# Which of four weight buffers each multiply of a feed-forward part reads: in turn, or 0, 1, 2, 3, 1, 2, 3

## The chip, the cores and the metric

The kernel runs on one core of one Trainium2 chip. The metric is the device time of one execution in microseconds (us); less is better. The engines are named PE (TensorE), DVE (VectorE), ACT (ScalarE), POOL (GpSimd) and SP (SyncE, which here only issues transfers).

## The reference

One layer of a decoder with 512 tokens and a width of 1024. A token mixer (forgetting attention beside a state-space branch, joined by gates) comes first; the change lies behind it, in the SwiGLU part:

```python
x = layer_norm(DEEPNORM_ALPHA * x + mixed, ln1_g[l], ln1_b[l])
h = (jax.nn.silu(x @ w_ffn_gate[l]) * (x @ w_ffn_up[l])) @ w_ffn_down[l]
x = layer_norm(DEEPNORM_ALPHA * x + h, ln2_g[l], ln2_b[l])
```

`w_ffn_gate` and `w_ffn_up` are 1024 x 2816, `w_ffn_down` is 2816 x 1024, all float32.

## The kernel before, in words

**Splits.** A float32 product is made of three faster ones. `split` (lines 103 and 104) makes of a tile a high part (a cast on ACT, `...h`) and a low part (the rest, a subtraction on DVE, `...l`). `mm3` (lines 145 to 147) issues high x high, high x low and low x high.

**The feed-forward part.** The hidden width is cut into six blocks, five of 512 columns and one of 256. For each block the gate product and the up product are a `Gemm` object each (G0, U0 for the first block, up to G5, U5). A `Gemm` does a 2 x 2 block product with seven multiplies instead of eight: P1, P2, P6, P5, P7, P3, P4, in this order in the steady part. Each has its own right operand, made once from the transposed rows of x (`RIGHT`: B11, B21, NT2, NT1, T3, B22, T4), and its own weights: a quarter of the weight block, or a sum of quarters. The right operands are tiles of 128 x 1024, read in pieces of 128 x 256. One multiply is `nj` x 4 x 3 matmuls: 24 in the first five blocks, 12 in the sixth. There are 12 x 7 = 84 multiplies.

**The weights' way.** `load` (line 875) brings quarters from HBM into eight slots `rq`; where a sum of two quarters is wanted, POOL issues a second, accumulating load (line 877), or DVE adds (lines 883 and 885, for P6 and P3). `op` then splits the quarter into one of four buffers, each a pair `wh`, `wl`. `nops` counts the operations, and the buffer is the count modulo four. Buffers 0 and 1 lie in a pool that opens early (`wop0`), 2 and 3 in one that opens after the output projection (`wop1`). `W_OFF` (line 35) puts 192 bytes ahead of buffers 1 and 2, and none ahead of 0 and 3. A buffer may be written again when the multiply that read it is over.

**Order.** Engines other than SP and POOL follow what a scheduler makes of the code, which knows the buffers' dependencies. The opening is written out by hand: G0 and U0 take turns (numbers 0 to 13: G0 P1, G0 P2, U0 P1, U0 P2, G0 P5, U0 P5, G0 P6, U0 P6, G0 P7, G0 P3, G0 P4, U0 P7, U0 P3, U0 P4). From number 12 on a loop runs through `rest`, in which the split for a multiply is recorded two multiplies ahead of it (`AHEAD`). The numbers of G1 to U5 are 14 to 83; G5 and U5, numbers 70 to 83, are the halves.

**Behind it.** The down projection (`gemm_down`) loads `w_ffn_down` in chunks into `raw` (line 126) and splits them into `whi`, `wlo`. The `raw` tiles lie where slots of `rq` were, so that SP's first such load waits until the last split has read its slot.

Of the kernel before, what the change touches and what calls it, by code (L numbers as in the profile page):

```python
# [42 lines left out]
def tile_hybrid_decoder_layer(  # L43
# [47 lines left out]
    def offset(p_, n, nm):  # L91

        if n:
            p_.tile([P, n // 4], F32, name="off" + nm)
# [7 lines left out]
    def split(hi, lo, src):  # L102
        nc.scalar.copy(out=hi, in_=src)  # L103
        nc.vector.tensor_tensor(out=lo, in0=src, in1=hi.bitcast(F32), op=ALU.subtract)  # L104
# [725 lines left out]
    nops = [0]  # L830
# [18 lines left out]
    class Gemm:  # L849
# [29 lines left out]
        def op(self, p_):  # L879

            r = self.raw
            if p_ == "P6":
                nc.vector.tensor_tensor(out=r["a11"], in0=r["s1"], in1=r["a11"], op=ALU.add)
            elif p_ == "P3":
                nc.vector.tensor_tensor(out=r["a12"], in0=r["a11"], in1=r["a12"], op=ALU.add)
            t = r[{"P1": "a11", "P2": "a12", "P6": "a11", "P5": "s1", "P7": "s3", "P3": "a12", "P4": "a22"}[p_]]
            i = nops[0] % 4
            wp, off = wpools[i]
            if nops[0] < 4:
                offset(wp, off, f"w{i}")  # L890
            nops[0] += 1
            o = [wp.tile([P, 1024], F32R, name="w" + x, tag=f"w{x}{i}", bufs=1)[:, 0:4 * self.F] for x in "hl"]
            if nops[0] == 2:
                offset(wp, W_OFF[4], "we")
            split(*o, t)
            self.ops[p_] = [self.v(i) for i in o]
# [254 lines left out]
```

## Time and profile before

| | us |
|---|---|
| median of 3 runs | 1131.83 (1131.39 to 1133.82) |
| the profiled execution | 1133.8 |
| its span on the core | 1132.1 |

| engine | busy us | share of the span |
|---|---|---|
| PE | 1104.3 | 98% |
| DVE | 777.6 | 69% |
| ACT | 526.7 | 47% |
| POOL | 134.4 | 12% |

Time is counted from the start of the span. The feed-forward multiplies begin at 784 us, the down projection at 1002.5 us. A row of the timeline gives start, duration, engine, line, operation, `out<-in`, shape and a count; brackets hold the engine's idle time before it and what ended that. Tile names stand without buffer numbers: `wh` and `wl` are any of the four buffers. A matmul's duration reaches over the next one's start, since they are pipelined, so PE's pace is read from the starts.

### The profile page before, as it was taken

How to read it: one execution, taken by the hardware profiler on the slowest of the kernel's cores; microseconds unless marked ns; L12 is line 12 of the kernel's file. 1: busy time of each engine (PE TensorE's matmuls, PEld its weight loads, DVE VectorE, ACT ScalarE, POOL GpSimd, SP SyncE). 2: the span in 40 equal slices, each digit the busy share in tenths (PEclk: the TensorE clock that was granted, in tenths of full speed). 3: DMA queues.
4: the chain of work that ended last, by engine and by line, in shares of the span. 5: the costliest groups of instructions: out<-in, count | busy, mean ns of one | idle time of the engine just before them, and what ended most of it. 6: DMA issues, size and time to landing. Idle time of an engine off the chain costs nothing.

```text
span 1132.1 us, 15815 instructions
## 1 busy us (share of the span) xinstructions
PE 1104.3 (98%) x6086; PEld 942.8 (83%) x6086; DVE 777.6 (69%) x1223; ACT 526.7 (47%) x912; POOL 134.4 (12%) x165
## 2 busy tenths in 40 slices
PE   7999999999999999999999999999999999999996
PEld 5887778777787878888888888888999999988885
DVE  2679973885688473788778744556997777777326
ACT  2477764454442341567566544313654555453210
POOL 3003130020114000122110000011111111100001
PEclk9999999999999999999999999999999999999999
DMA  6353243243231333321222135381788787565212
GB/s 198 111 169 108 84 128 93 75 124 100 75 94 59 94 91 93 91 61 57 75 75 75 57 114 184 101 214 42 210 197 208 184 204 159 103 233 176 93 56 75
DMA packets 116059, 134.20 MB, mean 119 GB/s; under 512 B 5668, under 2 KB 94480, under 8 KB 115856
## 3 DMA queue, kind: packets, MB, share of 16 engines
q1 hardware_dynamic: 98896, 111.75, 32.3%
q0 software_dynamic: 14640, 14.10, 7.6%
q10 hardware_dynamic: 2448, 7.34, 1.9%
q8 instruction: 48, 0.79, 0.3%
q14 instruction: 27, 0.22, 0.1%
HBM read 128.78 MB, written 4.26 MB: 118 GB/s over the span
## 4 chain that ended last, share of the span: by engine, by line
PE 80%; DVE 9%; issue 4%; DMA 3%; POOL 2%; ACT 2%; POOLq 0%; DVEq 0%; ACTq 0%
PE gps L147 19%; PE gps L146 19%; PE gps L145 19%; PE cps L146 5%; PE cps L147 5%; PE cps L145 4%; PE cps L509 2%; DVE wlo L104 2%; PE cps L370 1%; PE cps L499 1%; ACT whi L103 1%; DMA rq<-in_w_ffn_up_dram 1%; PE cps L474 1%; PE cps L475 1%; PE cps L328 1%
## 5 line engine op out<-in xcount | busy, mean ns | idle before, releaser
L104 DVE TENSOR_TENSOR wlo<-raw,whi 128x1024 fp32r<-128x1024 f32 x127 | 156.2, 1230 | 176.4 <-ACT whi L103 175.1
L103 ACT CAST whi<-raw 128x1024 fp32r<-128x1024 f32 x127 | 133.5, 1051 | 244.3 <-PE gps L146 97.8
L145 PE MATMUL gps<-xh,whi 128*128 128x512 f32 x456 | 180.9, 397 | 0.0
L147 PE MATMUL gps<-xh,wlo 128*128 128x512 f32 x456 | 179.6, 394 | 0.0
L146 PE MATMUL gps<-xl,whi 128*128 128x512 f32 x456 | 179.3, 393 | 0.0
L103 ACT CAST wh<-rq 128x1024 fp32r<-128x1024 f32 (+1 forms) x84 | 82.1, 979 | 94.5 <-PE cps L146 42.7
L104 DVE TENSOR_TENSOR wl<-rq,wh 128x1024 fp32r<-128x1024 f32 (+1 forms) x84 | 94.8, 1132 | 29.5 <-ACT wh L103 29.3
L147 PEld LDWEIGHTS gps<-xh,wlo 128*128 128x128 f32 x456 | 86.1, 189 | 17.5
L145 PEld LDWEIGHTS gps<-xh,whi 128*128 128x128 f32 x456 | 86.0, 189 | 17.3 <-issue 0.2
L146 PEld LDWEIGHTS gps<-xl,whi 128*128 128x128 f32 x456 | 86.0, 189 | 17.3 <-issue 0.2
L145 PE MATMUL gps<-whi,xh 128*128 128x512 f32 x192 | 76.3, 398 | 1.9 <-ACT whi L103 1.6
L146 PE MATMUL gps<-wlo,xh 128*128 128x512 f32 x192 | 75.6, 394 | 1.2 <-DVE wlo L104 1.2
L147 PE MATMUL gps<-whi,xl 128*128 128x512 f32 x192 | 75.5, 393 | 0.0
L282 DVE SCALAR_TENSOR_TENSOR t_v<-gps,cw,t_v 128x511 f32<-128x511 f32 (+2 forms) x72 | 53.4, 744 | 3.8 <-ACT t_v L279 3.1
L146 PE MATMUL gps<-t_ul,whi 128*128 128x512 f32 x128 | 51.1, 399 | 0.0
L147 PE MATMUL gps<-t_uh,wlo 128*128 128x512 f32 x128 | 51.0, 399 | 0.0
L145 PE MATMUL gps<-t_uh,whi 128*128 128x512 f32 x128 | 50.5, 395 | 0.0
L481 ACT ACTIVATE t_y<-t_y,sm 128x128 f32<-128x128 f32 (+1 forms) x64 | 35.6, 558 | 21.1 <-DVE sm L479 21.0
L145 PEld LDWEIGHTS gps<-whi,xh 128*128 128x128 f32 x192 | 36.4, 190 | 10.5 <-ACT whi L103 2.3
L146 PEld LDWEIGHTS gps<-wlo,xh 128*128 128x128 f32 x192 | 36.4, 190 | 9.4 <-DVE wlo L104 2.0
L364 ACT ACTIVATE t_ab<-t_ab,acum 128x128 f32<-128x128 f32 x128 | 41.6, 391 | 4.7 <-DMA t_ab<-ac_d 2.7
L147 PEld LDWEIGHTS gps<-whi,xl 128*128 128x128 f32 x192 | 36.3, 189 | 8.5 <-DVE xl L104 1.1
(567 smaller groups left out, 2717.0 us busy)
## 6 DMA issues: line engine op xcount, KB each, us to landing
raw<-in_w_in_dram SPq DMA_DIRECT2D x80, 512.0 KB, 3.7
rq<-in_w_ffn_gate_dram SPq DMA_DIRECT2D x25, 512.0 KB, 5.9
rq<-in_w_ffn_up_dram SPq DMA_DIRECT2D x25, 512.0 KB, 6.3
raw<-in_w_ffn_down_dram SPq DMA_DIRECT2D x22, 512.0 KB, 3.8
t_ab<-ac_d SPq DMA_DIRECT2D x32, 256.0 KB, 3.2
raw<-in_w_proj_ssm_dram SPq DMA_DIRECT2D x16, 512.0 KB, 3.5
rq<-in_w_ffn_gate_dram POOLq DMA_DIRECT2D x10, 512.0 KB, 8.4
rq<-in_w_ffn_up_dram POOLq DMA_DIRECT2D x10, 512.0 KB, 6.2
```

What stands on the lines that cost most here:

```text
L103: nc.scalar.copy(out=hi, in_=src)
L104: nc.vector.tensor_tensor(out=lo, in0=src, in1=hi.bitcast(F32), op=ALU.subtract)
L145: nc.tensor.matmul(out=o, lhsT=l[0], rhs=r[0], start=start, stop=False, skip_group_check=skip)
L146: nc.tensor.matmul(out=o, lhsT=l[0], rhs=r[1], start=False, stop=False, skip_group_check=skip)
L147: nc.tensor.matmul(out=o, lhsT=l[1], rhs=r[0], start=False, stop=stop, skip_group_check=skip)
L282: nc.vector.scalar_tensor_tensor(out=v[:, sh:], in0=ps[:, 0:T - sh], scalar=cw[:, k, blk:blk + 1], in1=v[:, sh:], op0=ALU.mult, op1=ALU.add)
L328: nc.tensor.transpose(out=pt[:, c * P:(c + 1) * P], in_=xst[:, c * P:(c + 1) * P], identity=ident)
L364: nc.scalar.activation(out=m[:, r, :], in_=m[:, r, :], func=AF.Relu, scale=-1.0, bias=acum[:, c, h:h + 1])
L370: nc.tensor.matmul(out=py[:, r * 64:(r + 1) * 64], lhsT=ms[r // 4][:, r % 4, :], rhs=xdt[:, r * 64:(r + 1) * 64], start=True, stop=True)
L474: nc.tensor.matmul(out=ps[:, 0:n], lhsT=q1[:, qs], rhs=k1[:, 0:n], start=True, stop=False)
L481: nc.scalar.activation(out=pt[:, 0:n], in_=pt[:, 0:n], func=AF.Exp, scale=-1.0, bias=sm[:, 2:3], accum_out=sm[:, 0:1])
L509: nc.tensor.matmul(out=po[:, kb * P:], lhsT=vt[:, kb, hh, :], rhs=pT[kb][j], start=kb == 0 and j == 0, stop=kb == NT - 1 and j == 1)
```

## The change

The buffer of an operation is no longer its count modulo four. With seven operations to a `Gemm`, the pattern has its period: P1 gets buffer 0, P2, P6 and P5 get 1, 2, 3, and P7, P3 and P4 get 1, 2, 3 again.

```diff
@@ -884,7 +884,7 @@
             t = r[{"P1": "a11", "P2": "a12", "P6": "a11", "P5": "s1", "P7": "s3", "P3": "a12", "P4": "a22"}[p_]]
-            i = nops[0] % 4
+            i = (0, 1, 2, 3, 1, 2, 3)[nops[0] % 7]
             wp, off = wpools[i]
             if nops[0] < 4:
                 offset(wp, off, f"w{i}")
```

The scheduler sees other dependencies and so places some instructions anew. ACT, in the opening, from the split of B11 and B21 on (`b11h`, `nt1h`, `b22h`, `nt2h` are high parts of right operands, line 982 normalises rows):

```order
 L103 CAST b11h<-xf 128x1024
 L103 CAST b21h<-xf 128x1024
-L103 CAST wh<-rq 128x1024 x3
-L900 COPY cp<-gps 128x512
-L103 CAST wh<-rq 128x1024
+L103 CAST wh<-rq 128x1024 x2
+L900 COPY cp<-gps 128x512
+L103 CAST wh<-rq 128x1024 x2
 L982 ACTIVATE xf<-cps,lnv 128x128 x8
 L952 ACTIVATE g<-cp 128x512
 L103 CAST wh<-rq 128x1024
 L900 COPY cp<-cps 128x512
+L103 CAST nt1h<-T 128x1024
```

The cast of `nt1h` now stands right behind the copy, ahead of that of `b22h`, which it followed. DVE at the same place (lines 1037 and 1040 make NT1 and NT2, lines 986 and 987 normalise, line 953 is a gate's evacuation):

```order
-L953 SCALAR_TENSOR_TENSOR g<-g,cp 128x512
+L1037 TENSOR_TENSOR T<-xf 128x1024
 L987 TENSOR_TENSOR xf<-xf,lnv 128x4x128
-L1037 TENSOR_TENSOR T<-xf 128x1024
-L104 TENSOR_TENSOR wl<-rq,wh 128x1024
+L953 SCALAR_TENSOR_TENSOR g<-g,cp 128x512
 L1040 SCALAR_TENSOR_TENSOR T<-T,xf 128x1024
 L104 TENSOR_TENSOR nt1l<-T,nt1h 128x1024
```

The low part `wl` that leaves this place is that of U0's P5. It comes back as the first of three behind `nt2l` and the product of line 959. In PE's row the first four matmuls of G0's and U0's P6 now stand behind the first two of U0's P5, which do not need that low part. PE at the start of the down projection (`T` is the hidden tile, `whi` and `wlo` the first chunk):

```order
 L146 MATMUL cps<-t4l,wh 128x256
 L147 MATMUL cps<-t4h,wl 128x256
-L145 MATMUL cps<-whi,T 128x512 x3
+L145 MATMUL cps<-whi,T 128x512 x4
+L146 MATMUL cps<-wlo,T 128x512
+L147 MATMUL cps<-whi,T 128x512
+L145 MATMUL cps<-whi,T 128x512
```

Four matmuls that need only the high part of the chunk now stand ahead of the first that needs its low part, instead of three.

## Rows read from the trace of the kernel before

**Rows 1.** Span and granted clock of the core.

```profile
core 0: 1132.1 us, clock 0.996
```

**Rows 2.** Stretches: length, busy time of each engine, clock, DMA share, GB/s.

```profile
core 0: us, PE busy (x) PEld busy (x) DVE busy (x) ACT busy (x) POOL busy (x), PEclk, DMA share, GB/s
...
804.00:830.00 26.00, 26.00 (x227) 26.00 (x226) 26.00 (x29) 16.02 (x20) 2.58 (x2) 1.00 0.84 211
830.00:983.00 153.00, 153.00 (x1332) 153.00 (x1332) 119.85 (x130) 79.21 (x97) 21.85 (x17) 1.00 0.75 178
...
1002.50:1110.00 107.50, 107.22 (x474) 88.47 (x474) 51.10 (x48) 30.58 (x30) 0.00 (x0) 1.00 0.41 136
```

**Rows 3.** PE's waits, 784 to 1016 us: total, times, longest.

```profile
PE gps L146 <- DVE nt1l L104: 1.0, 1, 1.0
PE cps L979 <- DVE t_sd L971: 0.9, 1, 0.9
PE gps L145 <- ACT nt1h L103: 0.6, 1, 0.6
PE cps L146 <- DVE wlo L104: 0.3, 1, 0.3
```

**Rows 4.** PE by stretch, cut at the starts of multiplies 15, 16, 18 and 20.

```profile
831.42:834.14 2.72, 2.72 (x26) 1.00 0.63 165
834.14:837.02 2.88, 2.88 (x26) 1.00 1.21 218
...
839.74:842.46 2.72, 2.72 (x26) 1.00 1.21 229
...
845.18:848.06 2.88, 2.88 (x26) 1.00 0.16 55
```

**Rows 5.** Timeline of ACT, then DVE, from 837 us: splits of weights.

```profile
837.15 1.05 ACT L103 CAST wh<-rq 128x1024 fp32r<-128x1024 f32 x1 [0.48 <-PE gps L146]
...
838.23 1.23 DVE L104 TENSOR_TENSOR wl<-rq,wh 128x1024 fp32r<-128x1024 f32 x1 [0.50 <-ACT wh L103]
840.95 1.23 DVE L104 TENSOR_TENSOR wl<-rq,wh 128x1024 fp32r<-128x1024 f32 x1 [1.50 <-ACT wh L103]
```

**Rows 6.** Timeline of ACT, DVE, SP and PE at the hand-over, 995 to 1004 us.

```profile
995.79 0.62 ACT L103 CAST wh<-rq 128x512 fp32r<-128x512 f32 x1 [0.47 <-ACT cp L900]
...
996.73 0.69 DVE L104 TENSOR_TENSOR wl<-rq,wh 128x512 fp32r<-128x512 f32 x1
...
997.45 1.90 SPq L126 DMA_DIRECT2D raw<-in_w_ffn_down_dram  x4
...
1001.31 1.05 ACT L103 CAST whi<-raw 128x1024 fp32r<-128x1024 f32 x1 [2.28 <-DMA raw<-in_w_ffn_down_dram]
...
1002.39 1.23 DVE L104 TENSOR_TENSOR wlo<-raw,whi 128x1024 fp32r<-128x1024 f32 x1
...
1002.54 0.86 PE L145 MATMUL cps<-whi,T 128*128 128x512 f32 x3
1003.68 0.50 PE L146 MATMUL cps<-wlo,T 128*128 128x512 f32 x1 [0.28 <-DVE wlo L104]
```

**Rows 7.** Timeline of ACT, DVE and PE in the opening, 797 to 801 us.

```profile
797.35 1.05 ACT L103 CAST b22h<-xf 128x1024 fp32r<-128x1024 f32 x1
798.30 1.04 ACT L103 CAST nt1h<-T 128x1024 fp32r<-128x1024 f32 x1
...
797.37 1.22 DVE L104 TENSOR_TENSOR wl<-rq,wh 128x1024 fp32r<-128x1024 f32 x1
798.51 1.22 DVE L1040 SCALAR_TENSOR_TENSOR T<-T,xf 128x1024 f32<-128x1024 f32 x1
799.64 1.22 DVE L104 TENSOR_TENSOR nt1l<-T,nt1h 128x1024 fp32r<-128x1024 f32 x1
800.78 0.69 DVE L903 TENSOR_TENSOR cp<-cps,cp 128x512 f32<-128x512 f32 x1
801.38 1.22 DVE L104 TENSOR_TENSOR nt2l<-T,nt2h 128x1024 fp32r<-128x1024 f32 x1
...
799.39 0.39 PE L145 MATMUL gps<-nt1h,wh 128*128 128x256 f32 x1 [0.63 <-ACT nt1h L103]
...
800.92 0.39 PE L146 MATMUL gps<-nt1l,wh 128*128 128x256 f32 x1 [1.02 <-DVE nt1l L104]
```

## The prediction, made before the change was run

> **What bounds the kernel now.** I read the core's span first [rows 1]: 1132.1 us at a granted clock of 0.996, so TensorE (PE) stands at its higher level, 2.4 GHz, nearly throughout. Then the busy time by stretch [rows 2]. From 804 us to the end of the feed-forward multiplies PE is busy without a gap; VectorE (DVE) is too from 804 to 830 us, and then has about a fifth free. After 1002.5 us PE lacks only 0.28 us of 107.50. So PE bounds this part, and a change counts only if it alters PE's pace or a PE wait. The list of PE's waits between 784 and 1016 us is short [rows 3]: 0.9 us for the normalised rows, which the change does not touch; 1.0 us and 0.6 us in the opening, for the low and high part of NT1; 0.3 us where the down projection starts.
>
> What remains is PE's pace. The windows cut at the starts of multiplies are to be read by their length [rows 4]. A multiply is 24 matmuls. Those at 831.42 and 839.74 take 2.72 us (113.3 ns a matmul), those at 834.14 and 845.18 take 2.88 us (120 ns). Both are 100% busy at clock 1.00. Counting operations from G0's P1 as number 0, the multiply at 834.14 is number 16 and that at 845.18 number 20: multiples of four, the ones that read buffer 0. I went through the starts of all 84 multiplies. The 21 on buffer 0 all run at 120 ns, with every right operand and both PSUM pools; 59 others run at 113, and four in the opening stretch at 118. It is not the load of the transfers: rows of 2.72 us stand at 165 and 229 GB/s, around one of 2.88 us at 218 [rows 4].
>
> **Part 1, fewer multiplies on the slow buffer.** Of 84 operations, numbers 0 to 69 have 24 matmuls and numbers 70 to 83 have 12. Before, buffer 0 holds 0, 4, ..., 80: 18 full ones and three halves (72, 76, 80). Now it holds 0, 7, ..., 77: ten full and two halves (70, 77). A full one costs 2.88 - 2.72 = 0.16 us too much, a half 0.08. Before 18 x 0.16 + 3 x 0.08 = 3.12 us, now 10 x 0.16 + 2 x 0.08 = 1.76 us. PE has no gap there, so the whole difference is on the path: **-1.36 us**. The bounds are 0, if the pace goes with a place in the turn and not with the buffer, and 1.36.
>
> The Trainium skill speaks against this term. Its page SBUF — State Buffer, section Who interferes with whom, says that only the port pair that VectorE shares with GpSimd causes contention and that PE never waits on anyone in SBUF; by it the buffer would not matter and the term would be 0. The rows differ, 2.88 against 2.72 us, and no neighbour's work runs in every fourth multiply alone, so I take the rows. The other reading is a rival below.
>
> **Part 2, a shorter lead.** Pattern 0, 1, 2, 3, 1, 2, 3 gives buffers 1 to 3 again after three operations for P7, P3 and P4, after four for P2, P6 and P5. Today the cast of a split starts when the last reader of its buffer ends: the cast at 837.15 (number 20) comes 0.13 us after multiply 16 ended at 837.02 [rows 4, 5]; its low part starts at 838.23 and is done at 839.46, for a multiply that starts at 845.18, 5.7 us to spare. With a distance of three the cast waits for multiply 17, 2.72 us later, and 3.0 us are left. In the half operations a lead of four multiplies becomes one of three (1.36 us less), where cast 0.62 and low part 0.69 [rows 6] must fit in the 2.72 us of two multiplies. Queued behind a later cast on ScalarE (ACT) are only evacuations. **0**, hidden by that lead, and no gain either, since PE waits for no split there; if the lead went, a full multiply would lose up to the 2.3 us of a whole split. Slots of the raw weights come free later by as much; no cast here waits for such a load, so nothing for that.
>
> **Part 3, the opening (797 to 806 us).** The order on ACT now has the high part of NT1 before that of B22, and DVE does NT1's low part before the low part of U0's P5. In today's times [rows 7]: nt1h can start at 797.35 instead of 798.30 and is done at 798.39, before PE has finished U0's P2 (799.39 less the wait of 0.63 is 798.76), so the 0.63 us go. The low part, now at 799.64, moves up by the 1.13 us between the DVE rows at 797.37 and 798.51; PE goes on at 800.92 - 1.13 = 799.79. What is late next is the moved split. After nt1l (from 798.51 on) DVE has an add of 0.60 (800.78 to 801.38), nt2l of 1.13 and h of 0.60, and nt2l must also await its own high part, which ends at 800.30 (ACT, after nt1h and b22h, 0.95 apart). So 800.3 + 1.13 + 0.60 = 802.05, and the split ends 1.22 later, 803.27. PE meanwhile has 23 matmuls of G0's P5 and five others before the first that needs it: 799.79 + 28 x 0.113 = 802.96. A new wait of 0.3 us stands there, and the gain is 1.13 - 0.3 = **-0.85 us**. Bounds: 0, if the new wait takes all, and -1.65, if both old waits (0.63 + 1.02) go and none comes. I stay with the sum, as each link has a row.
>
> **Part 4, the hand-over to the down projection.** SyncE (SP) issues the first load of the down weights at 997.45, when the split of the last block's P3 (U5's, number 82) has read the slot that the load fills: cast 995.79, low part 996.73 to 997.42 [rows 6]. The load lands 3.84 us later, its cast starts at 1001.31, the low part ends at 1003.62; PE starts the down projection at 1002.54 without delay and waits 0.28 us for that low part. Number 82 uses buffer 2 in both kernels, but its predecessor there was 78 and is now 79: one half multiply later, 1.36 us. Cast 997.15, low part 997.8 (it need not queue) to 998.5, load 998.5, landing 1002.35, cast done 1003.4. PE starts 0.9 us late. The low part is there at 1004.65. The order has four high-only matmuls before it instead of three, 0.9 us, so they end at 1004.3 and the next is issued at 1004.7, where before the same matmul (the second after the wait) came at about 1004.0. **+0.8 us**, rounding up. Bounds: 0 if the load lands faster, +1.36 if the whole delay shows. PE is busy to 1110 us [rows 2], so nothing is won back later.
>
> **Sum.** -1.36 - 0.85 + 0.8 = -1.4 us. The profiled execution took 1133.8 us (span 1132.1), so 1132.4 by its own time; it lies 2.0 us above the median of the three runs, 1131.83, and for the median I forecast **1130.4 us**. A measurement of this kernel can tell about 0.2% (2.3 us) from no change, so this counts as the same.
>
> **Rivals.** (a) The hand-over is free: with parts 1 and 3 alone 1131.83 - 2.2 = 1129.6, on the line to "faster". For it: the load need only land in 3.0 us instead of 3.84, since its cast would then end at 998.5 + 3.0 + 1.05 = 1002.55; against: it leads its queue in both kernels. Both opening waits gone with the hand-over paid gives the same 1129.6. Together 0.22.
>
> (b) The pace goes with something that comes every fourth multiply and not with the buffer: part 1 falls away, 1131.83 - 0.85 + 0.8 = 1131.8. Against it: the pattern holds through blocks in which the neighbours differ. By the rule quoted above it would be so. 0.10.
>
> (c) Slower: DVE falls behind in the opening stretch. From 804 to 830 us it has no idle time [rows 2], so each time it waits for a cast that comes a multiply later is lost. Later in the trace it waits 0.50 and 1.50 us for such casts [rows 5], 1.0 on average. If numbers 11 to 13 and 18 to 20 each cost it one multiply (2.72 us) less the 1.0 it can spend, 6 x 1.7 = 10.3 us are lost; the leads absorb the first 5.7 (spare above), so PE would lose 4.6 us: 1135.0. It decides from a lateness above 5.7 us; above 7.1 the kernel is slower than before. Against it: other splits stand ready in the queue. The Trainium skill warns of this (Perfetto Trace Analysis, Optimization Strategy: gaps that repeat on the engine that should be full can mean too few buffers); before the change no such gap is in the rows. 0.06.
>
> The forecast itself has 0.62.
>
> **How the numbers follow.** The likeliest case is 1130.4, with its own bounds from 1131.83 - 1.36 - 1.65 = 1128.8 to 1131.83 - 1.36 + 1.36 = 1131.8. Rivals (a) and (b) lie inside. The range is 1128.8 to 1132.2, which leaves (c) out and allows 0.4 us for the spread of the median (1131.39 to 1133.82 before). Faster by over 0.2% is below 1129.6: half of (a) and some of the forecast's edge, 0.20. Slower by over 0.2% is (c), 0.05. Same 0.75.
>
> **What would show it.** In the profile after: 2.88 us once in seven multiplies, at P1, and 2.72 for the rest; PE's wait for nt1h gone and that for nt1l smaller, with a new one for the low part of U0's P5; a first down matmul that waits about 0.9 us for the cast of the first load; DVE's waits for casts longer, without a PE wait behind them. A PE wait for wh or wl inside the blocks after 830 us would prove part 2 wrong; multiplies of 2.88 us on other buffers would prove part 1 wrong.

## The result, and the profile after

The change made the kernel slower. Run in turns on one chip, the kernel before took 1133.63 us and the changed one 1143.45 us (medians of 5 runs each, 1131.39 to 1134.11 and 1141.92 to 1145.31): a ratio of 1.0091, interval 1.0080 to 1.0102. The forecast of 1130.4 us and its whole range lie below that, and the median of the kernel before, which is 1.8 us higher with two more runs beside the three shown ahead, explains little of it. The profiled execution of the changed kernel took 1142.53 us.

First the core's span and clock, which answer to [rows 1]:

```profile
core 0: 1140.8 us, clock 0.998
```

The clock is the same, the span 8.7 us longer. The stretches, in the columns of [rows 2] (the last one is moved by 8.9 us, to the start of the down projection):

```profile
804.00:830.00 26.00, 26.00 (x223) 26.00 (x222) 26.00 (x28) 15.80 (x19) 3.79 (x3) 1.00 0.82 217
830.00:983.00 153.00, 146.93 (x1263) 146.15 (x1262) 112.91 (x122) 76.07 (x94) 19.33 (x16) 1.00 0.75 174
1011.40:1118.90 107.50, 107.41 (x473) 88.65 (x473) 50.95 (x47) 30.68 (x30) 0.00 (x0) 1.00 0.40 136
```

The opening and the down projection are as full as they were. The blocks are not: TensorE (PE) was busy for all of the 153 us from 830 to 983, now it is idle for 6.1 of them, and VectorE (DVE) does 6.9 us less work in the same stretch. The list of PE's waits, 784 to 1016 us (total, times, longest), which answers to [rows 3]:

```profile
PE gps L145 <- ACT cp L900: 4.3, 3, 1.5
PE gps L147 <- DVE wl L104: 2.0, 1, 2.0
PE cps L147 <- DVE wl L104: 1.3, 1, 1.3
PE cps L145 <- ACT whi L103: 1.0, 1, 1.0
PE cps L979 <- DVE t_sd L971: 0.9, 1, 0.9
PE gps L146 <- DVE nt1l L104: 0.7, 1, 0.7
```

The first three lines are new: five waits inside the blocks, 7.6 us. Two are for the low part of a split (`wl`), three for ScalarE's (ACT's) copy of a bank that PE adds to next (`cp`, line 900). What both stand behind is seen in the list of DVE's own waits, 804 to 1010 us; of these two lines the kernel before has neither:

```profile
DVE rq L883 <- DMA rq<-in_w_ffn_up_dram: 13.9, 5, 3.7
DVE rq L883 <- DMA rq<-in_w_ffn_gate_dram: 8.6, 3, 4.5
```

Line 883 is the sum for P6. Before, its ten instances in that stretch waited 0.3 us together; now eight of them wait 22.5 us for a load. One of them, in the timeline of DVE from 850 us on:

```profile
852.45 1.22 DVE L104 TENSOR_TENSOR wl<-rq,wh 128x1024 fp32r<-128x1024 f32 x1 [1.00 <-ACT wh L103]
858.13 1.22 DVE L883 TENSOR_TENSOR rq<-rq 128x1024 f32<-128x1024 f32 x1 [4.46 <-DMA rq<-in_w_ffn_gate_dram]
859.27 0.68 DVE L903 TENSOR_TENSOR cp<-cps,cp 128x512 f32<-128x512 f32 x1
859.88 1.22 DVE L104 TENSOR_TENSOR wl<-rq,wh 128x1024 fp32r<-128x1024 f32 x1
```

The matching rows of ACT and POOL, and then PE's matmul that was held:

```profile
851.37 1.05 ACT L103 CAST wh<-rq 128x1024 fp32r<-128x1024 f32 x1 [1.28 <-PE cps L146]
854.14 1.05 ACT L103 CAST wh<-rq 128x1024 fp32r<-128x1024 f32 x1 [1.23 <-issue]
...
849.02 1.28 POOL L877 DMA_DIRECT2D rq<-in_w_ffn_gate_dram  x1 [13.77 <-DVE wl L104]
...
861.14 0.39 PE L147 MATMUL cps<-t3h,wl 128*128 128x256 f32 x1 [1.30 <-DVE wl L104]
```

The cast at 851.37 and the low part at 852.45 are the split of the next Gemm's P1, into buffer 0. The cast at 854.14 is that of P7, which PE needs first. Its low part could start at 855.2; it starts at 859.88, because in DVE's queue the sum stands ahead of it, and the sum waits for the accumulating load issued at 849.02, which lands at 858.04. PE reaches the first matmul that reads this low part and stops until 861.14. The evacuation at 859.27 (line 903) is held as well: where ACT's product of a gate (line 952) and then its copy of the next bank come late by it, PE stops at P7's first matmul instead, as in the other three waits.

Why the sum stands there shows in the kernel before:

```profile
850.91 1.05 ACT L103 CAST wh<-rq 128x1024 fp32r<-128x1024 f32 x1 [1.18 <-issue]
...
859.18 1.05 ACT L103 CAST wh<-rq 128x1024 fp32r<-128x1024 f32 x1 [1.34 <-PE cps L146]
...
860.27 1.23 DVE L104 TENSOR_TENSOR wl<-rq,wh 128x1024 fp32r<-128x1024 f32 x1 [1.65 <-ACT wh L103]
861.53 1.22 DVE L883 TENSOR_TENSOR rq<-rq 128x1024 f32<-128x1024 f32 x1
```

There the cast of P7 comes at 850.91 and that of P1 three splits later, at 859.18, when its buffer has been read out; the sum follows at 861.53 without a wait, 4.6 us after its load landed (856.89). In the changed kernel P1's buffer is number 0, which nobody else uses once the opening is over (there, with G0 and U0 taking turns, number 7 is U0's P6 and not a P1). It stands free, so the scheduler issues P1's split three places early, and behind it the sum, which overwrites the quarter that P1's split reads and so could not go before it.

To set the parts side by side I measured every interval between the starts of two matmuls from the first feed-forward multiply to the first down matmul, and sorted them against 113.3 ns (us; the last two columns are kernels of the next section):

| | before | after | late_sum | late_sum_82 |
|---|---|---|---|---|
| 1848 matmuls at 113.3 ns | 209.44 | 209.44 | 209.44 | 209.44 |
| excess of those at 119 to 126 ns (nearly all on buffer 0) | 3.12 | 2.01 | 1.79 | 1.87 |
| excess of those at about 118 ns | 0.37 | 2.72 | 0.45 | 0.45 |
| gaps in the opening, up to 804 us (16 transposes of 2.0 us stand in them) | 5.34 | 4.48 | 4.47 | 4.47 |
| gaps in the blocks | 0.05 | 8.93 | 0.00 | 0.00 |
| gap at the hand-over to the down projection | 0.00 | 1.19 | 0.86 | 0.00 |
| sum | 218.3 | 228.8 | 217.0 | 216.2 |

The sum grew by 10.4 us: 8.9 in the blocks' gaps, 2.4 by the second pace, 1.2 at the hand-over, less 1.1 for buffer 0 and 0.9 in the opening. (The span grew by 8.7, since the profiled execution before began its feed-forward part 1.6 us later.) The three paces stand side by side in three multiplies of the changed kernel, numbers 26, 28 (on buffer 0) and 29, in the columns of [rows 2]:

```profile
863.85:866.67 2.82, 2.82 (x26) 2.82 (x25) 2.64 (x4) 1.05 (x1) 0.00 (x0) 1.00 0.78 247
869.50:872.37 2.87, 2.87 (x26) 2.87 (x25) 2.50 (x4) 1.05 (x1) 1.28 (x1) 1.00 0.51 129
872.37:875.09 2.72, 2.72 (x26) 2.72 (x25) 1.23 (x1) 1.53 (x2) 0.37 (x1) 1.00 1.11 200
```

### The profile page after: what moved, and what is told of

It reads as the page before. It is cut to its first block, busy times and chain, and to the rows that moved or that the text cites. A ratio compares the mean times of both kernels' runs of the same rounds, so it can differ in the third digit from the quotient of the medians.

```text
span 1140.8 us, 15820 instructions
## 1 busy us (share of the span) xinstructions
PE 1105.2 (97%) x6086; PEld 942.9 (83%) x6086; DVE 777.3 (68%) x1223; ACT 525.5 (46%) x912; POOL 134.2 (12%) x165
## 4 chain that ended last, share of the span: by engine, by line
PE 76%; DVE 10%; issue 5%; DMA 4%; POOL 2%; ACT 2%; POOLq 0%; DVEq 0%; ACTq 0%
PE gps L147 18%; PE gps L146 18%; PE gps L145 18%; PE cps L147 4%; PE cps L146 4%; PE cps L145 4%; PE cps L509 2%; DVE wlo L104 2%; DMA rq<-in_w_ffn_up_dram 1%; PE cps L370 1%; PE cps L499 1%; ACT whi L103 1%; DVE wl L104 1%; PE cps L474 1%; DMA rq<-in_w_ffn_gate_dram 1%
```

## The experiments

Two theories stood against each other. **Theory 1**: the sum, moved ahead of its load, blocks DVE's queue. **Theory 2**: three buffers in turn are too few, and the splits themselves come late. All ratios are to the kernel before, run in turns on the same chip.

**late_sum.** The changed kernel, with the sum queued behind the low part of P2's split (`split` returns its subtraction here; `c0` is 0 in the first block, which stays as it is):

```diff
-                nc.vector.tensor_tensor(out=r["a11"], in0=r["s1"], in1=r["a11"], op=ALU.add)
+                with tc.issue_after(self.last[-1].ins) if self.c0 else ExitStack(): nc.vector.tensor_tensor(out=r["a11"], in0=r["s1"], in1=r["a11"], op=ALU.add)
...
-            split(*o, t)
+            self.last.append(split(*o, t))
```

> The changed kernel, with the sum of P6 (L883) queued on VectorE behind the subtraction of P2's split, and nothing else held; from block 1 on. Theory 1 (the sum was moved ahead of the landing of its accumulating load, and everything behind it on VectorE waits with it): VectorE's idle time at L883 before a DMA falls from 22.5 us to under 3, the five TensorE gaps of 1.6 to 2.3 us (8.4 us together) go, and with them most of the 638 matmuls at 118 ns (2.4 us), so 0.990 to 0.993 of the changed kernel, which is 0.998 to 1.001 of the kernel before. Theory 2 (three buffers in turn are too few, the splits themselves come late): gaps of the same size stay, 1.006 to 1.011 of the kernel before.

Measured: 1130.73 us, ratio 0.9996 (0.9987 to 1.0004). PE's waits:

```profile
PE cps L979 <- DVE t_sd L971: 0.9, 1, 0.9
PE gps L146 <- DVE nt1l L104: 0.7, 1, 0.7
PE cps L145 <- ACT whi L103: 0.7, 1, 0.7
```

All five waits in the blocks are gone, and DVE's for line 883 too. PE's order is that of the changed kernel. P1's split still runs ahead into buffer 0; its cast and, some 13 us later, the low part of P2's split and the sum:

```profile
847.23 1.06 ACT L103 CAST wh<-rq 128x1024 fp32r<-128x1024 f32 x1 [1.10 <-PE cps L146]
...
859.63 1.22 DVE L104 TENSOR_TENSOR wl<-rq,wh 128x1024 fp32r<-128x1024 f32 x1
860.77 1.22 DVE L883 TENSOR_TENSOR rq<-rq 128x1024 f32<-128x1024 f32 x1
```

The cast at 847.23 follows the end of multiply 21 (847.14), the last reader of buffer 0; the buffer of P7's split was then still being read. Only where DVE issues the sum, and what follows from that in DVE's and ACT's order, differs. So theory 1 holds, and the whole loss of the change hung on this one place.

**splits_in_turn.** The sum is free again, but each split's cast and subtraction are queued behind those of the split before:

```diff
-            split(*o, t)
+            st_ = ExitStack(); [st_.enter_context(tc.issue_after(x.ins)) for x in (self.last[-1] if self.c0 else ())]; self.last.append(split(*o, t)); st_.close()
```

> The changed kernel, with every split's cast and subtraction from block 1 on queued behind those of the split before it, so that P1's split can't be taken out of its turn into buffer 0; the sum is free to go where it likes behind P1's split. Theory 1 as refined (buffer 0 stands free for seven multiplies, so P1's split and the sum that only waits for it are issued three splits early): the sum falls back into its place, 0.997 to 1.001 of the kernel before. Theory 2 (three buffers in turn are too few): stays at 1.006 to 1.011, since the buffers are used as in the changed kernel.

Measured: 1132.03 us, ratio 1.0000 (0.9992 to 1.0009), no wait in the blocks. Buffers are used as in the changed kernel, so theory 2 falls. What lets the sum go early is P1's split running ahead; late_sum shows that by itself this does no harm.

**no_second_half.** The load for which the sum waits is cut instead:

```diff
-                for s_ in src[nm][1:]:
+                for s_ in src[nm][1:] if nm != "s1" or not self.c0 else ():
```

> The changed kernel without the accumulating load of s1 from block 1 on: the second quarter of the weights that belongs into s1 is left out, so the sum's operand lands with its first load, some 8 to 9 us earlier. Theory 1 (the sum waits for the accumulating load): VectorE's wait at L883 goes, gaps of 1.6 us and more go, 0.996 to 1.002 of the kernel before. Theory 2 (three buffers): 1.006 to 1.011, nothing of the splits' order is mended by it.

Measured: 1131.74 us, ratio 0.9991 (0.9982 to 1.0001); DVE no longer waits at line 883, and PE has no wait in the blocks. ACT and DVE execute the changed kernel's instructions in the changed kernel's order here, so the sum still stands early; with the accumulating load out of the way that costs nothing. The three kernels cut the chain at three places, at the split, at the sum and at the load, and each cut brings the loss back whole.

**buffer0_moved.** This one tests part 1 of the forecast in the kernel before:

```diff
-HB_OFF, B_OFF, W_OFF, D_OFF = 512, 160, (0, 192, 192, 0, 320), (0, 0, 0, 160)
+HB_OFF, B_OFF, W_OFF, D_OFF = 512, 160, (192, 0, 192, 0, 320), (0, 0, 0, 160)
```

> The kernel before with buffer 0 moved by 192 bytes (W_OFF's first number 0 -> 192, the second 192 -> 0, so everything else stays where it was); no instruction changes place. Place theory (a multiply takes 2.88 us from buffer 0 and 2.72 from the others because of where buffer 0 lies): 18 full and 3 half multiplies at 2.72 and 1.36, 3.1 us less, 0.997 of the kernel before. Rival (each fourth multiply is slow whatever its buffer): no change, 0.999 to 1.001. Second rival (the slow multiply is what ends the pace of 118 ns that follows a gap; in the kernel before it has 87 such matmuls, in the changed one 638): the multiplies settle at 118 ns, 2.83 us, slower by up to 1848 x 4.7 ns = 8.6 us less 3.1, up to 1.005.

Measured: 1137.58 us, ratio 1.0046 (1.0034 to 1.0058): the second rival. Four of its multiplies, as in [rows 4] but with PE alone (length, busy, clock, DMA share, GB/s); the second and the fourth read buffer 0, the first buffer 3, the third buffer 1:

```profile
851.36:854.19 2.83, 2.83 (x27) 1.00 0.98 314
854.19:857.01 2.82, 2.82 (x26) 1.00 0.99 162
857.01:859.84 2.83, 2.83 (x26) 1.00 1.12 330
865.50:868.32 2.82, 2.82 (x26) 1.00 1.16 240
```

No multiply takes 2.88 us any more, so the 120 ns did go with the place of buffer 0. But they do not come down to 2.72 us either: 82 of the 84 run at 118 ns, whatever their buffer; the other two, in the opening between two gaps, run at 113.3.

**three_in_turn, three_in_turn_82, late_sum_moved.** The next three ask what the second pace is, and at the same time test theory 1 once more and the hand-over. The first two leave buffer 0 after the fourteenth split, the second uses it once more for split 82, the third is late_sum with buffer 0 moved as above:

```diff
-            i = (0, 1, 2, 3, 1, 2, 3)[nops[0] % 7]
+            i = (0, 1, 2, 3, 1, 2, 3)[nops[0] % 7] if nops[0] < 14 else 1 + (nops[0] - 14) % 3
```

```diff
-            i = (0, 1, 2, 3, 1, 2, 3)[nops[0] % 7]
+            i = (0, 1, 2, 3, 1, 2, 3)[nops[0] % 7] if nops[0] < 14 else 1 + (nops[0] - 14) % 3 if nops[0] != 82 else 0
```

> The changed kernel with its seven-place pattern for the first 14 splits alone and buffers 1, 2, 3 in plain turn from the 15th on: the sum is held by nothing, but P1's split has no free buffer to run ahead into. Theory 1: the sum stands in its old place, no TensorE gap between 830 and 995 us. Theory of the pace (a gap can leave the matmuls at 118 ns, and a slow multiply from buffer 0 brings them back to 113.3; the one at 806 us, behind the last gap of the opening, is enough): all multiplies after it at 2.72 us, the 8 full and 2 half multiplies at 2.88 and 1.44 us of late_sum become 2.72 and 1.36, 1.4 us under late_sum, 0.997 to 0.9985 of the kernel before. If the pace needs a slow multiply every so often: 118 ns returns, up to 1848 x 4.7 ns = 8.6 us more, 1.002 to 1.006. Theory 2 (three buffers in turn are too few): every wait of the changed kernel and more, 1.006 to 1.015.

> As three_in_turn, with split 82, the last but one, in buffer 0, which is long free. The forecast's reading of the hand-over (the first raw weights of the down projection come one half multiply later because split 82 waits for buffer 2) expects the gap of 1.0 to 1.3 us at the last matmul back at 0.1 to 0.4, and so 0.6 to 1.1 us under three_in_turn less 0.08 for one half multiply from buffer 0; 0.996 to 0.998 of the kernel before. Rival: the gap is set by a later buffer or load and stays, the same as three_in_turn.

> late_sum with buffer 0 moved by 192 bytes as in buffer0_moved: no slow multiply anywhere, no gap after the opening. Theory of the pace: 118 ns from the last gap of the opening to the end of the multiplies, some 1700 x 4.7 ns = 8.0 us more, less the 1.3 us of the slow multiplies: 1.004 to 1.007 of the kernel before. Rival (the 118 ns of buffer0_moved came from something in the turn of the buffers, not from a missing slow multiply): 1.3 to 1.8 us under late_sum, 0.998.

Measured: three_in_turn 1133.31 us, ratio 1.0009 (0.9990 to 1.0028); its twelve runs form two groups, six from 1128.8 to 1131.1 and six from 1135.6 to 1138.9 (the next expectation counts seven and five), and the median lies between them. three_in_turn_82 1129.84 us, ratio 0.9995 (0.9977 to 1.0014), again two groups: eight from 1128.5 to 1129.9, four from 1135.2 to 1137.3. late_sum_moved 1137.66 us, ratio 1.0044 (1.0032 to 1.0056), as the theory of the pace said. In none of them is there a wait in the blocks, and the first two have no hold on the sum at all: with three buffers in plain turn P1's split has nowhere to run ahead to. The gap at the hand-over was 1.51 us from start to start in three_in_turn and nothing over a matmul in three_in_turn_82, so split 82 is what it hangs on. The two groups were not expected.

**three_again_1, three_again_2.** three_in_turn twice more, for the profile of one of its long runs.

> three_in_turn once more, for a profile of one of its long runs (5 of its 12 runs took 1135.6 to 1138.9 us, 7 took 1128.8 to 1131.1). Theory of the pace: in a long run the matmuls change from 113.3 to 118 ns at one place behind 808 us and stay there, with no gap of over 1 us new; 7 us are some 1500 matmuls x 4.7 ns. Rival: the long runs have gaps, or a lower granted clock. A short run tells nothing new.

> A third look at three_in_turn, for the same purpose as three_again_1: in a long run the theory of the pace expects 118 ns from one place to the end of the multiplies, the rival gaps or a lower granted clock.

The first took 1130.43 us, the second 1137.68: a long run. PE from 808 to 983 us, in the columns of the last windows, in three_again_2 and in the short run of three_in_turn:

```profile
808.00:983.00 175.00, 175.00 (x1488) 1.00 0.75 181
```

```profile
808.00:983.00 175.00, 175.00 (x1545) 1.00 0.78 184
```

Both are full, both at clock 1.00, without a gap. One does 1488 instructions in 175 us (117.6 ns each), the other 1545 (113.3). The long run went over to 118 ns at the wait for NT1's low part, which ended at 799.08 us, and the multiply on buffer 0 at 807.87 did not end it; after that none came. So the theory of the pace held in kind, but one slow multiply is not always enough.

**late_sum_82.** That asks for a slow multiply now and then, and for split 82 in buffer 0:

```diff
-            i = (0, 1, 2, 3, 1, 2, 3)[nops[0] % 7]
+            i = (0, 1, 2, 3, 1, 2, 3)[nops[0] % 7] if nops[0] != 82 else 0
```

with the two edits of late_sum.

> late_sum with split 82 in buffer 0, the rest of the pattern as in the changed kernel: buffer 0 is used each seventh time to the end. Theory of the pace: no group of runs 7 us above the rest, since a slow multiply comes each 19 us and ends whatever set the matmuls to 118 ns. Forecast's hand-over: the gap of 0.97 us at the last matmul goes to about 0.1, 0.8 us under late_sum: 0.998 to 0.9995 of the kernel before.

Measured: 1130.06 us, ratio 0.9979 (0.9970 to 0.9988), one group of eleven runs, 1129.11 to 1131.66. PE starts the down projection without a gap and waits only for the chunk's low part:

```profile
999.69 1.18 PE L145 MATMUL cps<-whi,T 128*128 128x512 f32 x4
1001.50 0.50 PE L146 MATMUL cps<-wlo,T 128*128 128x512 f32 x1 [0.63 <-DVE wlo L104]
```

By the ratio it is 0.21% (2.4 us) faster than the kernel before, and so faster than both kernels of this case; a little more than was expected. In the traces split 82 itself brings less than was expected: the gap of 0.86 us goes, but the wait of 0.63 us for the low part comes in its place, and from the first feed-forward multiply to the hundredth down matmul late_sum_82 takes 0.2 us less than late_sum. Why the ratios of the two differ by more is open.

## Why the prediction was wrong

**The step that failed is part 2**, the shorter lead: "0, hidden by that lead, and no gain either, since PE waits for no split there", and its last sentence, "no cast here waits for such a load, so nothing for that". It looked at the buffers that come back sooner, with distances of three and four, and there it was right: splits_in_turn and three_in_turn use three buffers in turn and PE waits for none. It did not look at the buffer that comes back later. Buffer 0 now rests for seven operations, and a resource that is free earlier lets its next user be issued earlier. What then came along was not a cast but the sum on DVE, which needs P1's split to be over and a load to have landed. In the kernel before that sum had 4.6 us to spare after the landing; at the head of the queue by 853.67 us instead of 861.53 it had none, and the queue behind it stood for up to 4.46 us at a time. The place of line 883 in DVE's order was there to be read beside the change; I read the order in the opening and at the hand-over only. The price was 8.9 us of gaps and 2.4 us of the second pace. The forecast named a PE wait for `wl` inside the blocks as what would prove this part wrong, and two such waits are in the list.

That DVE does not pass a waiting instruction is told by the Trainium skill as well: PSUM — Partial Sum Buffer, section Engine vs sequencer instructions, calls the queues of ScalarE, VectorE and GpSimd strict FIFO. The trace agrees: P7's low part had its input at 855.2 us and stood behind the sum until 859.88.

**Part 1** (-1.36 us) was right in kind and size where the blocks run clean: 3.12 us fell to 1.79 in late_sum, -1.33. In the changed kernel the row gives -1.11, because strays of the 118 ns pace count in it; on the multiplies of buffer 0 alone it is -1.4, and the matmuls at 118 ns took more than that gave. Its reading that buffer 0 is slow because of the buffer and not of the place in the turn is shown by buffer0_moved; rival (b) falls. What it did not see is that the slow buffer also does something useful.

**Part 3** (-0.85 us) measured -0.87 in late_sum and -0.86 in the changed kernel. The wait for NT1's high part is gone, that for the low part is 0.7 us instead of 1.0, and the forecast's new delay at the low part of U0's P5 is there too: in the changed kernel 0.33 us lie between two of PE's starts, 801.44 and 801.77, 0.2 us more than the pace.

**Part 4** (+0.8 us) measured 0.86 in late_sum and 1.19 in the changed kernel at the first down matmul; 0.14 of either comes back within the next fifty, where the wait for the low part [rows 3] is gone. That it hangs on split 82 is shown by late_sum_82 and three_in_turn_82, where the gap is gone. Rival (a), a free hand-over, falls.

The sum of the forecast, -1.4 us, is what the trace of late_sum shows in its feed-forward part: 217.0 against 218.3 us. By its ratio of 0.9996 late_sum is only 0.5 us faster than the kernel before, with an interval that reaches to 1.5 us. **Rival (c)** had the right sign. Its place was the opening, where DVE has no idle time, its mechanism late casts, its price 4.6 us; but from 804 to 830 us PE is as full after as before [rows 2], and the loss came later, where DVE had a fifth of its time free.

## What to carry to other kernels

When a change lets one buffer rest longer, list what the scheduler can now issue earlier because of it, and check each such instruction against the landing of every load that it needs: on an in-order queue one early instruction with a late operand holds all that stands behind it. An engine with a fifth of its time free is no cover against that, since what counts is the order of its queue and not its load. Before a slow operand is taken out, look at what its slowness does for its neighbours, and time several runs, as a median can hide two groups.

## What was not expected of the hardware

Matmuls of one shape (128x256) ran at three paces with the granted clock at 1.00 and no wait in the rows: 113.3, 118 and 120 ns from start to start.

The 120 ns belongs to where buffer 0 lies: moved by 192 bytes, it is gone (buffer0_moved, late_sum_moved). The Trainium skill, SBUF — State Buffer, section Who interferes with whom, has only the port pair of VectorE and GpSimd as a cause of contention. The runs here show a loss that this does not cover: the same instructions in the same order ran at 120 ns from one place and never from the other. Why that place is slower was not settled.

The 118 ns belongs to no buffer. In the twelve traces of this case the pace went over from 113.3 to 118 ns 17 times, always at a gap of PE; behind three gaps it stayed at 113.3. In the two kernels with buffer 0 moved the very first multiply ran at 118 ns, with no gap before it. The pace stays for any length: 79 of 84 multiplies in three_again_2, 82 of 84 in buffer0_moved, all 84 in late_sum_moved. It ended only at another gap or at a multiply on buffer 0. Of 16 slow multiplies that followed one at 118 ns without a gap, 11 were followed by 113.3 ns; of 64 that followed one at 113.3, none by 118. So in the kernel before buffer 0 costs 3.1 us and guards against up to 1848 x 4.7 ns = 8.7 us, which would explain why taking its slowness away made that kernel slower by 0.46%. The rival, that buffer 0 sets off the 118 ns from its new place, was not tested apart; three_again_2 speaks for the first reading, since it kept 118 ns to the end with buffer 0 where it was and not used after the opening. What sets the pace inside the engine was not tried.
